# Attention scores from scaled fp16 halves, and one size bound for latent and context inputs

## The chip, the cores and the metric

The kernel runs on one core of one Trainium2 chip. The metric is the time of one execution on the device in microseconds; of several runs the median is taken. Engine names in profile rows: PE is TensorE's matmul, PEld its weight load, DVE VectorE, ACT ScalarE, POOL GpSimd, SP SyncE, which issues DMAs.

## The reference

One layer of a diffusion backbone over 1024 latent tokens with a prefix of 256 context tokens, 1024 channels, all inputs and the output in fp32. A modulated RMS norm and one wide projection feed two token mixers; their outputs are gated, merged and projected, and a ConvFFN follows. What the change touches is the attention mixer: 16 query heads of width 64 in 4 groups, each group with one key and one value head, a window of 128 latent tokens to either side, all 256 context keys, and one learned sink logit per head.

```python
q = apply_rope(rms_norm(heads(aq, ATT_HEADS, ATT_HEAD_DIM), q_norm_w[l]), cos, sin)
k = apply_rope(rms_norm(heads(ak, ATT_KV_HEADS, ATT_HEAD_DIM), k_norm_w[l]), cos, sin)
v = heads(av, ATT_KV_HEADS, ATT_HEAD_DIM)
k_ctx = rms_norm(heads(akc, ATT_KV_HEADS, ATT_HEAD_DIM), k_norm_w[l])
v_ctx = heads(avc, ATT_KV_HEADS, ATT_HEAD_DIM)
...
s_lat = jnp.einsum('btkgd,bskd->bkgts', qblk, kblk).astype(jnp.float32) * ATT_SCALE
s_lat = jnp.where(valid, s_lat, NEG_INF)
s_ctx = jnp.einsum('btkgd,bskd->bkgts', qblk, k_ctx).astype(jnp.float32) * ATT_SCALE
p = jax.nn.softmax(jnp.concatenate([s_lat, s_ctx, sink_b], axis=-1), axis=-1).astype(v.dtype)
return (jnp.einsum('bkgts,bskd->btkgd', p[..., :3 * T], vblk)
        + jnp.einsum('bkgts,bskd->btkgd', p[..., 3 * T:3 * T + C], v_ctx))
```

The other mixer is a chunkwise mLSTM in both directions; it, the merge and the ConvFFN follow the attention in time and are not touched.

## The kernel before

**Products.** The kernel reaches fp32 accuracy with narrower products: each operand is split into a high and a low half (`split_from`: ScalarE writes the high half, VectorE subtracts it from the source for the low one), and three products (high-high, high-low, low-high) are summed in PSUM. In some places the halves are in fp32r, a form of fp32 that TensorE multiplies in one pass; in others they are fp16, and then the operand is first multiplied by a factor that keeps it within fp16's range. Weights get their factor from the sum of their squares (`ScaledWeights.square`, `total`, `back`; `f[:, 2:3]` is the factor, `f[:, 4:5]` its inverse together with that of the inputs). The normalised inputs `hT` (latent) get theirs from a bound on their size (`size_bound`, result in `E.hs`), worked out from the modulation vectors.

**Stages.** `stage_startup` loads the modulation weights, normalises context and latent tokens, forms the context keys and values (`context_keys`, `context_values`, `context_squares`) and the mLSTM's context inputs (the loop over `i` in 0..3, tiles `cx`, `kvx`), and prepares the loop's first weights. The order of its instructions is set by a planner that ranks them by estimated times; `issue_after` pins single ones. `stage_attention` is one loop whose order is written out by hand (`manual_schedule`): step `n` projects block `n` of 32 (4 head groups of 8 blocks of 128 queries, tile `pq`), turns block `n-1` (transposes on TensorE, tile `qt`, into `QT` and `KA`/`KB`), forms scores and softmax of block `n-3` (`Scores`: `product`, `top`, `exps`, `low` for each of four heads `h`) and multiplies block `n-4`'s probabilities with the values (`po`). Between these stands filler work for TensorE: half a tile of gate projection per step (`g`). GpSimd splits the weights of later steps (`split_pool`) and VectorE sums the modulation rows (`macc`). `stage_mlstm` and `stage_tail` follow; the planner orders them.

**Scores.** The query tile `QT` holds, per head, the high half of 64 channels on 64 partitions and the low half on the other 64; the keys `KA` hold the high half twice and `KB` the low half twice. Two matmuls over 128 partitions (L860, L861) then sum all four products, for up to 384 latent keys; L862 and L863 do the same for 256 context keys with `KcA` and `KcB`. All four have the same stationary slice of `QT`. The result lies in one of two score banks (`s`, 1024 columns each). On it VectorE adds the mask with the row factor `ss` and takes the extreme (`top`, L868), ScalarE exponentiates twice (`exps`, L878 into fp16, L879 in place), and VectorE subtracts the two (`low`, L884), after which the bank is free.

**Factors of a head group.** `weight_back(g)` finishes the factors for group `g` three steps into the group before (group 0 ahead of the loop). It calls `back` (a reciprocal on VectorE, L126, and a product on GpSimd, L127). Then it forms, on GpSimd, the factor `up` that latent and context values of the group share. It is the inverse square root of a sum of the inputs' and the context values' squares (`at.vq`, from `context_squares`); L690 is the power. VectorE takes its reciprocal as `down` (L692). `values_act` and `values_dve` use `upi` to write the value halves; `context_values` uses `up`; `norm_row` uses `down` for the normaliser.

**Handover from startup to loop.** The loop's pools reuse the memory of the startup's pools. A tile waits until what lay there has been read. The gate weights' raw pieces (`fr`, L697) are among the first; their squares (L112) and the sum over partitions on TensorE (L119) stand ahead of the first gate tile.

Of the kernel before, what the change touches and what calls it, by code (L numbers as in the profile page):

```python
# [8 lines left out]
F32 = mybir.dt.float32  # L9
F32R = mybir.dt.float32r  # L10
# [8 lines left out]
P = 128  # L19
D = 1024  # L20
L = 1024
# [279 lines left out]
def attention_setup(E, st):  # L301
# [6 lines left out]
    qw = ap.tile([P, 2, HD], F32, name="qw")  # L308
# [3 lines left out]
    def constants():  # L312
        nc.sync.dma_start(qw[:, 0], A["q_norm_w"].to_broadcast([P, HD]))
        nc.sync.dma_start(qw[:, 1], A["k_norm_w"].to_broadcast([P, HD]))
        nc.gpsimd.tensor_scalar(qw[:, 0], qw[:, 0], -(HD ** -0.5), None, op0=ALU.mult)
# [17 lines left out]
    KcA = ap.tile([P, NKV, NCTX], F32R, name="KcA")  # L333
    KcB = ap.tile([P, NKV, NCTX], F32R, name="KcB")
    Vcf = ap.tile([P, NCB, NKV * HD], F32, name="Vcf")
    vq = ap.tile([P, NKV], F32, name="vq")
    at.__dict__.update(maskA=maskA, nsink=nsink, sink=sink, qw=qw, TA=TA, TB=TB, KcA=KcA, KcB=KcB, Vcf=Vcf, vq=vq, constants=constants, tables=tables)
# [3 lines left out]
def stage_startup(E, at):  # L341
# [3 lines left out]
    with ExitStack() as st:  # L345
# [128 lines left out]
        def k_stack(kf, nh, name):  # L474
            w = nh * HD
            kk = wp.tile([P, 512], F32, tag="kk", name=f"kk{name}", bufs=1)
            kh = kk[:, : 2 * w].rearrange("p (h r d) -> p h r d", r=2, d=HD)
            kv = kf.rearrange("p (h d) -> p h d", d=HD)
            for r in range(2):
                copy_act(nc, kh[:, :, r].bitcast(F32R), kv)  # L480
            kl = wp.tile([P, 512], F32, tag="kl", name=f"kl{name}", bufs=1)
            kl4 = kl[:, : 2 * w].rearrange("p (h r d) -> p h r d", r=2, d=HD)
            for r in range(2):
                nc.vector.tensor_tensor(kl4[:, :, r].bitcast(F32R), kv, kh[:, :, r], op=ALU.subtract)
            return kk, kl

# [44 lines left out]
        def context_squares():  # L531
            q = sp.tile([P, NKV], F32, name="vsq")
            for g in range(NKV):
                junk = sp.tile([P, P], F32, name=f"vj{g}", tag="vj").rearrange("p (a b) -> p a b", a=2)
                nc.scalar.activation(junk, at.Vcf[:, :, g * HD : (g + 1) * HD], AF.Square, accum_out=q[:, g : g + 1])
            pb = tp_tile("vq")
            nc.tensor.matmul(pb[:, :NKV], E.ones, q, start=True, stop=True)
            nc.vector.tensor_scalar(at.vq, pb[:, :NKV], 2.0 ** -30, None, op0=ALU.mult)

        def context_keys():  # L540
            for c in range(NCB):
# [13 lines left out]
                nc.vector.tensor_tensor(kv4, kv4, at.qw[:, 1, None, :].to_broadcast([P, NKV, HD]), op=ALU.mult)  # L555
                kk, kl = k_stack(kf, NKV, f"c{c}")
                for src, dst in ((kk, at.KcA), (kl, at.KcB)):
                    pt = tp_tile(f"kct{c}")
                    for h in range(NKV):
                        nc.tensor.transpose(pt[:, h * P : (h + 1) * P], src[:, h * P : (h + 1) * P], ident)  # L560
                    copy_act(nc, dst[:, :, c * P : (c + 1) * P], pt.rearrange("p (h t) -> p h t", h=NKV))


        cs = sp.tile([P, NB, HD], F32, name="cs")
        for i in range(4):
# [48 lines left out]
            if i == 2:  # L614
                context_squares()
# [17 lines left out]
def stage_attention(E, st, at):  # L633
# [44 lines left out]
    def weight_back(g):  # L678
        f = RAW["wf", g]
        if g:  # L680
            w2.back(f)
        if g >= NKV:
            return
        t = wp.tile([P, 8], F32, tag="vs", name=f"vs{g}")
        inv = f[:, 4:5]
        nc.gpsimd.tensor_tensor(t[:, 0:1], inv, inv, op=ALU.mult)
# [3 lines left out]
        nc.gpsimd.tensor_tensor(t[:, 3:4], t[:, 2:3], expo[:, 0:1], op=ALU.pow)  # L690
        nc.gpsimd.tensor_tensor(t[:, 4:5], t[:, 3:4], inv, op=ALU.mult)
        nc.vector.reciprocal(t[:, 5:6], t[:, 3:4])  # L692
        G[g] = dict(inv=inv, inv2=t[:, 1:2], up=t[:, 3:4], upi=t[:, 4:5], down=t[:, 5:6])
# [58 lines left out]
    def values_act(g, b, ps):  # L752
# [3 lines left out]
        copy_act(nc, G[g]["V"][:, b, 0:HD], ps[:, 320:384], scale=G[g]["upi"])  # L756
        return sq

    def values_dve(g, b, ps, sq):
# [5 lines left out]
        nc.gpsimd.tensor_scalar(ss[:, :5], ss[:, :5], G[g]["inv"], None, op0=ALU.mult)  # L765
        V = G[g]["V"]
        nc.vector.scalar_tensor_tensor(
            V[:, b, HD:P], ps[:, 320:384], G[g]["upi"], V[:, b, 0:HD], op0=ALU.mult, op1=ALU.subtract
# [1686 lines left out]
```

## Time and profile before

| what | value |
|---|---|
| median of 3 runs | 1868.58 us (1866.38 to 1869.55) |
| profiled execution, its own time | 1870.95 us |
| its span, first to last instruction | 1869.2 us |
| instructions | 28015 |
| mean granted TensorE clock | 0.985 |
| attention loop, first to last score product | 137.7 to 614.5 us |
| score products L860 to L863 | 128 of each |
| fp32r weight load of `QT` / fp16 weight load of `hH` | 0.19 us / 0.10 us |

A row of instructions gives start, duration, engine, line, operation, the tiles written and read, shapes, and in brackets the idle time of the engine before it with what ended it. A row of groups gives a count, then the busy time in us and the mean of one in ns. Durations of matmuls overlap one another, so the pace of TensorE is read from starts.

### The profile page before, as it was taken

To read this page: it belongs to the slowest core of one execution; us is meant where nothing else is said; L and a number is where in the kernel's file an instruction comes from. 1 tells how busy PE (TensorE), PEld (TensorE's weight loads), DVE (VectorE), ACT (ScalarE), POOL (GpSimd) and SP (SyncE) were. 2 spreads that over 40 slices of the span, in tenths; PEclk is the share of its full clock that TensorE was granted. 3 is DMA by queue.
4 is the path that set the end of the run, shared out by engine and by line. 5 is a ranking of instruction groups with operands and counts; after the bars stand their busy time and mean duration, and the time that the engine had idled before them with its cause. 6 is when DMAs were issued, how large, how long until landed. Compare 5 with 4: busy or idle time off the path is not lost.

```text
span 1869.2 us, 28015 instructions
## 1 busy us (share of the span) xinstructions
PE 1802.4 (96%) x9217; PEld 1317.5 (70%) x9217; DVE 1419.8 (76%) x2870; ACT 1073.5 (57%) x2235; POOL 510.8 (27%) x750
## 2 busy tenths in 40 slices
PE   7889999999999799999999999999999999999999
PEld 3855555656665465757567887878888888888887
DVE  3847878777788585858687888689988898897665
ACT  4846777777777565554455564375544444455441
POOL 2476859577772530403020021000000000000000
PEclk9999999999999999998999999999999999999999
DMA  9646979978786826161439935422455444599751
GB/s 361 217 133 125 186 163 182 198 150 191 167 168 127 218 63 225 35 229 57 158 103 354 377 129 209 180 68 102 175 189 199 172 177 156 193 316 363 278 169 68
DMA packets 302194, 342.49 MB, mean 183 GB/s; under 512 B 176208, under 2 KB 200672, under 8 KB 299232
## 3 DMA queue, kind: packets, MB, share of 16 engines
q1 hardware_dynamic: 287648, 314.47, 55.9%
q10 hardware_dynamic: 14400, 26.22, 4.3%
q8 instruction: 73, 1.20, 0.3%
q14 instruction: 73, 0.60, 0.1%
HBM read 224.61 MB, written 76.16 MB: 161 GB/s over the span
## 4 chain that ended last, share of the span: by engine, by line
PE 79%; DVE 6%; issue 4%; ACT 4%; DMA 3%; POOL 3%; ACTq 0%; SPq 0%; POOLq 0%; DVEq 0%
PE g L724 8%; PE pq L724 7%; PE pa L2033 4%; PE pa L2034 4%; PE pa L2035 4%; PE po L724 3%; PE dx L2033 2%; PE dx L2035 2%; PE dx L2034 2%; PE pb L2034 2%; PE pb L2033 2%; PE pb L2035 2%; PE yb L2033 2%; PE yb L2034 2%; PE yb L2035 2%
## 5 line engine op out<-in xcount | busy, mean ns | idle before, releaser
L868 DVE CUSTOM_DVE_ANT_0 s<-s,maskA,nsink 128x640 f32<-128x640 f32 (+1 forms) x128 | 117.5, 918 | 84.4 <-PE s L863 83.7
L884 DVE TENSOR_TENSOR P<-s,P 128x640 f16<-128x640 f32 (+1 forms) x128 | 100.6, 786 | 0.8 <-ACT s L879 0.8
L878 ACT ACTIVATE P<-s,st 128x640 f16<-128x640 f32 (+1 forms) x128 | 98.2, 767 | 4.2
L724 PE MATMUL g<-hH,fh 128*128 128x512 f16 x256 | 98.3, 384 | 0.0
L724 PE MATMUL g<-hH,fl 128*128 128x512 f16 x256 | 98.0, 383 | 0.0
L724 PE MATMUL g<-hL,fh 128*128 128x512 f16 x256 | 97.8, 382 | 0.0
L879 ACT ACTIVATE s<-s,st 128x640 f32<-128x640 f32 (+1 forms) x128 | 93.8, 733 | 0.0
L876 ACT ACTIVATE st<-st,shift 128x1 f32<-128x1 f32 x128 | 37.6, 294 | 97.7 <-DVE st L868 96.7
L724 PEld LDWEIGHTS <-hH 128*128 128x128 f16 x640 | 60.6, 99 | 38.2 <-issue 2.9
L724 PE MATMUL pq<-wha,hH 128*128 128x384 f16 (+1 forms) x256 | 85.8, 335 | 0.0
L724 PE MATMUL pq<-wla,hH 128*128 128x384 f16 (+1 forms) x256 | 85.7, 335 | 0.0
L724 PE MATMUL pq<-wha,hL 128*128 128x384 f16 (+1 forms) x256 | 85.6, 334 | 0.0
L724 PEld LDWEIGHTS <-fh 128*128 128x128 f16 x512 | 45.9, 99 | 48.0 <-issue 1.6
L1442 POOL TENSOR_SCALAR kwh<-k,gcall 128x128 fp32r<-128x128 f32 x72 | 32.5, 455 | 166.2 <-ACT k L47 41.6
L2171 ACT ACTIVATE cv<-ua,vecT 128x1024 f32<-128x1024 f32 x22 | 27.4, 1245 | 86.2 <-DVE ua L2144 86.2
L860 PE MATMUL s<-KA,QT 128*128 128x384 f32 (+1 forms) x128 | 61.0, 477 | 10.8 <-DVE P L884 8.2
L2033 PE MATMUL dx<-dwh,dfh 128*128 128x512 f32 (+1 forms) x176 | 68.3, 388 | 0.0
L2035 PE MATMUL dx<-dwh,dfl 128*128 128x512 f32 (+1 forms) x176 | 68.3, 388 | 0.0
L2034 PE MATMUL dx<-dwl,dfh 128*128 128x512 f32 (+1 forms) x176 | 68.2, 387 | 0.0
L47 ACT ACTIVATE dfh<-drf 128x512 fp32r<-128x512 f32 x55 | 34.3, 628 | 58.5 <-PE dy L2034 25.6
L163 PE MATMUL kv<-whkv,hH 128*128 128x384 f16 x192 | 62.6, 326 | 4.7 <-DVE VL L56 4.7
L54 DVE TENSOR_TENSOR dfl<-drf,dfh 128x512 fp32r<-128x512 f32 x55 | 37.5, 688 | 34.3 <-ACT dfh L47 34.3
(694 smaller groups left out, 6335.5 us busy)
## 6 DMA issues: line engine op xcount, KB each, us to landing
ur<-in_w_up SPq DMA_DIRECT2D x22, 1024.0 KB
wmb<-in_w_modB SPq DMA_DIRECT2D x48, 256.0 KB
f_d<-cv SPq DMA_DIRECT2D x22, 512.0 KB
wm<-in_w_modA SPq DMA_DIRECT2D x16, 512.0 KB
fr<-in_w_g SPq DMA_DIRECT2D x32, 256.0 KB
drf<-fs_d SPq DMA_DIRECT2D x15, 512.0 KB
drw<-wt_d SPq DMA_DIRECT2D x14, 512.0 KB
w1b<-in_w_cx SPq DMA_DIRECT2D x16, 388.0 KB
```

The lines of the kernel that those rows point to most:

```text
L54: rest = nc.vector.tensor_tensor(lo, src, whole, op=ALU.subtract)
L163: nc.tensor.matmul(ps, lh[:, ls], rh[:, rs], start=start and i == 0, stop=False)
L724: nc.tensor.matmul(self.ps, x, w, start=self.i == 0, stop=self.i == self.n - 1)
L860: nc.tensor.matmul(s[:, self.lat], q, G[g]["KA"][:, ks], start=True, stop=False)
L868: nc.vector.tensor_tensor_reduce(e, e, self.mask, scale=self.ss[:, h : h + 1], scalar=nsink[:, hh : hh + 1], op0=ALU.add, op1=ALU.min, acc ...
L876: nc.scalar.activation(m, st4[:, 8 + h : 9 + h], AF.Identity, bias=shift)
L878: nc.scalar.activation(two[:, :W], e, AF.Exp, bias=m, scale=-1.0)
L879: nc.scalar.activation(e, e, AF.Exp, bias=m, scale=-1.0, accum_out=st4[:, 4 + h : 5 + h])
L884: nc.vector.tensor_tensor(two[:, W : 2 * W], self.e[h], two[:, :W], op=ALU.subtract)
L2033: nc.tensor.matmul(ps, lh, rh, start=start and i == 0, stop=False, skip_group_check=True)
L2034: nc.tensor.matmul(ps, lh, rl, start=False, stop=False, skip_group_check=True)
L2035: nc.tensor.matmul(ps, ll, rh, start=False, stop=stop and i == n - 1, skip_group_check=True)
```

## The change

Queries and keys become fp16 halves, the norm weights get factors for that in `constants`, the size bound covers context inputs as well, and the value factor no longer depends on the context values' squares.

- `constants` forms `wn`: sums of squares of the two norm weights (two ScalarE squares), their inverse square roots on GpSimd (a power over two columns), half the product of the two, and its reciprocal (VectorE). The query and key norm weights are multiplied with these and powers of two; `qw[:, 2]` is the one for context keys.
- `KcA`, `KcB`, `KA`, `KB` and `QT` are fp16 instead of fp32r. `context_keys` no longer stacks two fp32r halves and transposes both; it transposes the keys once and splits them out of PSUM with `split_from`.
- `size_bound` runs over 16 columns instead of 8 (scales and shifts of latent and context).
- `context_squares` and `at.vq` are gone. `weight_back` forms four small products on GpSimd; the power L690 and the reciprocal L692 are gone. The value scale `upi` becomes the constant 2^-15, and the row factor uses `invc`, which holds the norm weights' factor.

```diff
-    qw = ap.tile([P, 2, HD], F32, name="qw")
+    qw = ap.tile([P, 3, HD], F32, name="qw")
+    wn = ap.tile([P, 8], F32, name="wn")
...
-        nc.gpsimd.tensor_scalar(qw[:, 0], qw[:, 0], -(HD ** -0.5), None, op0=ALU.mult)
+        for i in range(2):
+            nc.scalar.activation(qw[:, 2], qw[:, i], AF.Square, accum_out=wn[:, i : i + 1])
+        nc.gpsimd.tensor_scalar(wn[:, 0:2], wn[:, 0:2], 1.0, 1e-36, op0=ALU.mult, op1=ALU.add)
+        nc.gpsimd.tensor_tensor(wn[:, 2:4], wn[:, 0:2], E.expo[:, 0:2], op=ALU.pow)
+        nc.gpsimd.tensor_scalar(wn[:, 4:5], wn[:, 2:3], wn[:, 3:4], 0.5, op0=ALU.mult, op1=ALU.mult)
+        nc.vector.reciprocal(wn[:, 5:6], wn[:, 4:5])
+        nc.gpsimd.tensor_scalar(qw[:, 0], qw[:, 0], wn[:, 2:3], -(2.0 ** -15), op0=ALU.mult, op1=ALU.mult)
+        nc.gpsimd.tensor_scalar(qw[:, 2], qw[:, 1], wn[:, 3:4], 2.0 ** 11, op0=ALU.mult, op1=ALU.mult)
+        nc.gpsimd.tensor_scalar(qw[:, 1], qw[:, 2], wn[:, 4:5], None, op0=ALU.mult)
...
-    KcA = ap.tile([P, NKV, NCTX], F32R, name="KcA")
-    KcB = ap.tile([P, NKV, NCTX], F32R, name="KcB")
+    KcA = ap.tile([P, NKV, NCTX], F16, name="KcA")
+    KcB = ap.tile([P, NKV, NCTX], F16, name="KcB")
...
-            sc = mods[:, 0].rearrange("p k -> p k")
-            nc.gpsimd.tensor_tensor(q[:, 8:16], sc, sc, op=ALU.mult)
-            nc.scalar.activation(q[:, 24:32], q[:, 8:16], AF.Square, accum_out=q[:, 0:1])
-            nc.scalar.activation(q[:, 24:32], mods[:, 2], AF.Square, accum_out=q[:, 1:2])
+            sc, sh = [mods[:, i : i + 2].rearrange("p s k -> p (s k)") for i in (0, 2)]
+            nc.gpsimd.tensor_tensor(q[:, 8:24], sc, sc, op=ALU.mult)
+            nc.scalar.activation(q[:, 24:40], q[:, 8:24], AF.Square, accum_out=q[:, 0:1])
+            nc.scalar.activation(q[:, 24:40], sh, AF.Square, accum_out=q[:, 1:2])
...
-                kk, kl = k_stack(kf, NKV, f"c{c}")
-                for src, dst in ((kk, at.KcA), (kl, at.KcB)):
-                    pt = tp_tile(f"kct{c}")
-                    for h in range(NKV):
-                        nc.tensor.transpose(pt[:, h * P : (h + 1) * P], src[:, h * P : (h + 1) * P], ident)
-                    copy_act(nc, dst[:, :, c * P : (c + 1) * P], pt.rearrange("p (h t) -> p h t", h=NKV))
+                kk = wp.tile([P, 512], F32, tag="kk", name=f"kkc{c}", bufs=1)
+                for r in range(2):
+                    copy_act(nc, kk.rearrange("p (h r d) -> p h r d", r=2, d=HD)[:, :, r], kv4)
+                pt = tp_tile(f"kct{c}")
+                for h in range(NKV):
+                    nc.tensor.transpose(pt[:, h * P : (h + 1) * P], kk[:, h * P : (h + 1) * P], ident)
+                cs_ = slice(c * P, (c + 1) * P)
+                split_from(nc, at.KcA[:, :, cs_], at.KcB[:, :, cs_], pt.rearrange("p (h t) -> p h t", h=NKV))
...
-            if i == 2:
-                context_squares()
...
-        nc.gpsimd.tensor_tensor(t[:, 0:1], inv, inv, op=ALU.mult)
-        nc.gpsimd.tensor_scalar(t[:, 1:2], t[:, 0:1], 1.0 / HD, None, op0=ALU.mult)
-        nc.gpsimd.tensor_scalar(t[:, 2:3], t[:, 0:1], 2.0 ** 30, at.vq[:, g : g + 1], op0=ALU.mult, op1=ALU.add)
-        nc.gpsimd.tensor_scalar(t[:, 2:3], t[:, 2:3], 1e-36, None, op0=ALU.add)
-        nc.gpsimd.tensor_tensor(t[:, 3:4], t[:, 2:3], expo[:, 0:1], op=ALU.pow)
-        nc.gpsimd.tensor_tensor(t[:, 4:5], t[:, 3:4], inv, op=ALU.mult)
-        nc.vector.reciprocal(t[:, 5:6], t[:, 3:4])
-        G[g] = dict(inv=inv, inv2=t[:, 1:2], up=t[:, 3:4], upi=t[:, 4:5], down=t[:, 5:6])
+        nc.gpsimd.tensor_scalar(t[:, 0:1], inv, inv, 1.0 / HD, op0=ALU.mult, op1=ALU.mult)
+        nc.gpsimd.tensor_tensor(t[:, 1:2], inv, at.wn[:, 5:6], op=ALU.mult)
+        nc.gpsimd.tensor_scalar(t[:, 2:3], f[:, 2:3], E.hs[:, 0:1], 2.0 ** -15, op0=ALU.mult, op1=ALU.mult)
+        nc.gpsimd.tensor_scalar(t[:, 3:4], inv, 2.0 ** 15, None, op0=ALU.mult)
+        G[g] = dict(inv=inv, inv2=t[:, 0:1], invc=t[:, 1:2], up=t[:, 2:3], down=t[:, 3:4])
...
-                KA=kp.tile([P, L], F32R, tag="KA", name=f"KA{g}"),
-                KB=kp.tile([P, L], F32R, tag="KB", name=f"KB{g}"),
+                KA=kp.tile([P, L], F16, tag="KA", name=f"KA{g}"),
+                KB=kp.tile([P, L], F16, tag="KB", name=f"KB{g}"),
...
-        copy_act(nc, G[g]["V"][:, b, 0:HD], ps[:, 320:384], scale=G[g]["upi"])
+        copy_act(nc, G[g]["V"][:, b, 0:HD], ps[:, 320:384], scale=2.0 ** -15)
...
-        QT = wp.tile([P, 512], F32R, tag="QT", name=f"QT{g}_{b}", bufs=3)
+        QT = wp.tile([P, 512], F16, tag="QT", name=f"QT{g}_{b}", bufs=3)
```

More of the change, by code (lines that the diff above doesn't have):

```diff
@@ L331, in tables @@
                 nc.gpsimd.tensor_tensor(TB[i][:, :, 32:64], sinb, w1, op=ALU.mult)
-    KcA = ap.tile([P, NKV, NCTX], F32R, name="KcA")
-    KcB = ap.tile([P, NKV, NCTX], F32R, name="KcB")
+    KcA = ap.tile([P, NKV, NCTX], F16, name="KcA")
+    KcB = ap.tile([P, NKV, NCTX], F16, name="KcB")
     Vcf = ap.tile([P, NCB, NKV * HD], F32, name="Vcf")
-    vq = ap.tile([P, NKV], F32, name="vq")
-    at.__dict__.update(maskA=maskA, nsink=nsink, sink=sink, qw=qw, TA=TA, TB=TB, KcA=KcA, KcB=KcB, Vcf=Vcf, vq=vq, constants=constants, tables=tables)
+    at.__dict__.update(maskA=maskA, nsink=nsink, sink=sink, qw=qw, TA=TA, TB=TB, KcA=KcA, KcB=KcB, Vcf=Vcf, wn=wn, constants=constants, tables=tables)
     return at
@@ L472, in stage_startup @@
         size_bound()
[L474 to L485, printed above, removed]
         def both(ps, w, n, ks):
@@ L529, in context_values @@
                     copy_act(nc, at.Vcf[:, c], pvc[c][:, :256])
[L531 to L538, printed above, removed]
         def context_keys():
```

10 lines of the change are left out of this document (5 added, 5 removed).

## The prediction

> **What bounds the kernel now.** I read the page first, then the stages by windows, then the waits inside the attention loop, then the instructions around the longest of them.
>
> ```profile
> span 1869.2 us, 28015 instructions
> ...
> PE 1802.4 (96%) x9217; PEld 1317.5 (70%) x9217; DVE 1419.8 (76%) x2870; ACT 1073.5 (57%) x2235; POOL 510.8 (27%) x750
> ...
> PE 79%; DVE 6%; issue 4%; ACT 4%; DMA 3%; POOL 3%; ACTq 0%; SPq 0%; POOLq 0%; DVEq 0%
> ```
>
> TensorE is busy for 96% of the span and carries 79% of the chain that ended last. So a microsecond counts where TensorE stands still, or where its own work gets shorter; the rest is hidden until it makes TensorE wait. The windows cut the span into startup, attention loop and everything after it (columns: length, busy time and count of PE, PEld, DVE, ACT and POOL, granted clock, DMA share, GB/s).
>
> ```profile
> 0.00:137.70 137.70, 114.20 (x629) 79.62 (x629) 77.18 (x159) 76.74 (x160) 61.89 (x94) 0.94 0.68 239
> 137.70:614.50 476.80, 459.11 (x2638) 279.96 (x2637) 372.94 (x962) 362.57 (x908) 327.37 (x402) 0.99 0.80 166
> 614.50:1869.20 1254.70, 1229.11 (x5955) 957.88 (x5953) 969.70 (x1750) 634.15 (x1168) 121.50 (x255) 0.99 0.52 184
> ```
>
> The change touches the first two stages. In the loop TensorE idles 476.8 - 459.1 = 17.7 us. The waits of that stage (us in total, times, longest) say what ends the idle time:
>
> ```profile
> DVE vs L692 <- POOL vs L690: 9.4, 3, 3.2
> ...
> PE s L860 <- DVE P L884: 8.2, 6, 2.0
> ```
>
> Both are one event, seen three times, once for each head group prepared inside the loop. `weight_back` ends in a reciprocal on VectorE (L692) of a power that GpSimd computes (L690). VectorE takes its work in order, so while the reciprocal waits, the score maximum behind it (L868) and the subtraction that frees a score bank (L884) stand too, and TensorE finds no bank. The middle event in time order (start, duration, and in brackets the idle time before):
>
> ```profile
> 270.99 0.15 DVE L126 RECIPROCAL wfa<-wfa 128x1 f32<-128x1 f32 x1
> 274.31 0.16 DVE L692 RECIPROCAL vs<-vs 128x1 f32<-128x1 f32 x1 [3.17 <-POOL vs L690]
> 274.43 0.82 DVE L868 CUSTOM_DVE_ANT_0 s<-s,maskA,nsink 128x512 f32<-128x512 f32 x1
> ...
> 272.44 0.19 POOL L686 TENSOR_TENSOR vs<-wfa 128x1 f32<-128x1 f32 x1
> ...
> 273.70 0.57 POOL L690 TENSOR_TENSOR vs<-vs,expo 128x1 f32<-128x1 f32 x1
> ...
> 271.10 0.28 PE L863 MATMUL s<-KcB,QT 128*128 128x256 f32 x1
> ...
> 276.00 0.41 PE L860 MATMUL s<-KA,QT 128*128 128x384 f32 x1 [2.02 <-DVE P L884]
> ...
> 153.44 0.66 PE L860 MATMUL s<-KA,QT 128*128 128x384 f32 x1 [1.99 <-DVE P L884]
> ...
> 393.81 0.41 PE L860 MATMUL s<-KA,QT 128*128 128x384 f32 x1 [2.01 <-DVE P L884]
> ```
>
> The reader is to see that the scores of the last head were ready at 271.10 + 0.28 = 271.4, that VectorE began on them at 274.43, and that TensorE lost 2.0 us each time. There is a second price, in the granted clock (column behind the five busy times):
>
> ```profile
> 152.80:159.60 6.80, 6.16 (x20) 3.64 (x21) 4.33 (x12) 4.16 (x10) 5.57 (x5) 0.50 0.75 157
> 272.30:275.70 3.40, 1.69 (x8) 0.59 (x6) 1.39 (x4) 0.32 (x2) 2.42 (x8) 1.00 0.16 40
> 391.75:395.20 3.45, 1.44 (x10) 1.11 (x10) 3.08 (x10) 2.01 (x5) 2.03 (x5) 1.00 0.09 18
> 395.20:398.60 3.40, 3.40 (x13) 1.80 (x12) 2.41 (x6) 2.17 (x6) 3.25 (x4) 0.50 0.94 245
> ```
>
> After the first and third stall TensorE worked at half clock, for 6.8 and 3.4 us.
>
> **The change part by part.** (a) *The factor of a head group (`weight_back`).* Six GpSimd instructions with a power become four without one, and no reciprocal follows on VectorE. The remaining reciprocal, L126 of `back`, had its input long before (0.15 us, no wait). VectorE then reaches L868 at about 271.4 instead of 274.43, the bank is freed 3.0 us earlier, and TensorE's 2.0 us are covered: 3 x 2.0 = **6.0 us**. The next thing late would be the scores themselves, TensorE's own work. The GpSimd queue also gets shorter, by about 1 us: from 272.44 to the power's end at 274.27 it runs five instructions and one more follows, against four short ones. The bound below is a gain of 0, if another operand of L868 came as late; its operands are the scores at 271.4, mask and sink from before the loop, and the row factors of an earlier step.
>
> (b) *The half clock behind the stalls.* Of 6.16 us busy at half clock half is lost, 3.1 us, and 1.7 of 3.4: together **4.8 us**. Ends: 0, if the clock falls for another reason, and 4.8. I take 4.8, since in both cases the idle stretch stands right ahead. The second stall was not followed by it, and the two windows say why it may not have been: TensorE was busy 1.69 us of the 3.4 before 275.7, and only 1.44 before 395.2. [...]
>
> (c) *The score products in fp16.* `Scores.product` issues four matmuls a head with the same stationary slice of `QT`. A typical block:
>
> ```profile
> 302.24 0.38 PE L724 MATMUL g<-hL,fh 128*128 128x512 f16 x1
> ...
> 304.40 0.38 PE L724 MATMUL g<-hH,fl 128*128 128x512 f16 x1
> 304.43 0.53 PE L860 MATMUL s<-KA,QT 128*128 128x384 f32 x1
> ...
> 305.09 0.28 PE L863 MATMUL s<-KcB,QT 128*128 128x256 f32 x1
> 305.21 0.34 PE L724 MATMUL pq<-wha,hH 128*128 128x384 f16 x1
> ...
> 307.33 0.33 PE L724 MATMUL pq<-wla,hH 128*128 128x384 f16 x1
> ...
> L861 PEld LDWEIGHTS s<-KB,QT 128*128 128x128 f32 x128 | 24.5, 192 | 2.1
> L724 PEld LDWEIGHTS <-hH 128*128 128x128 f16 x640 | 60.6, 99 | 38.2 <-issue 2.9
> ...
> 600.00:610.00 10.00, 8.65 (x58) 5.55 (x59) 9.93 (x19) 6.06 (x18) 9.59 (x7) 1.00 0.47 102
> ```
>
> Durations overlap, so starts are read. Ten 512-column fp16 products take 2.16 us, 0.216 each; thirteen of 384 columns (305.21 to 307.33) 2.12, 0.163 each. That is 0.41 ns a column, so 256 columns of fp16 would take 0.11. The block takes 305.21 - 304.40 - 0.216 = 0.594 us; in fp16 it would be 2 x 0.163 + 2 x 0.11 = 0.546. So today's format already streams at nearly the same rate, and the gain is 0.048 us a head, the 256-column products (0.12 each now) giving less than half of it. A quarter of the heads, first and last block of a group, have four 256-column products, for 4 x 0.01; so 0.045 on average. A weight load of fp16 takes 99 ns against 192 and would no longer be longer than the product it hides behind. All 128 heads would give 5.8 us; the last three steps (12 heads) lie where VectorE is full (9.93 of 10 us), so I count 116: **5.2 us**. Ends: 0, if what precedes a block and not the format costs the difference, and 128 x 0.06 = 7.7 us, if the block came down to its bare 1280 columns (0.53 us).
>
> (d) *ACT and VectorE in the loop.* The copies into `QT` and `KA` and the subtractions into `QT` and `KB` keep their count and shape and still read fp32 from PSUM; a scale that was a tile becomes a constant. I take 0; both engines have 100 us of idle time in this stage to cover a small change either way.
>
> (e) *Startup.* These rows carry it:
>
> ```profile
> L535 ACT ACTIVATE vj<-Vcf 128x128 f32<-128x128 f32 x4 | 1.2, 306 | 0.0
> L47 ACT ACTIVATE KcB<-kct 128x512 fp32r<-128x512 f32 x2 | 1.2, 592 | 0.0
> L484 DVE TENSOR_TENSOR klc<-kcf,kkc 128x256 fp32r<-128x256 f32 x4 | 1.5, 418 | 0.0
> 142.51 0.69 DVE L884 TENSOR_TENSOR P<-s,P 128x512 f16<-128x512 f32 x1
> 28.17 0.40 POOL L315 TENSOR_SCALAR qw<-qw 128x64 f32<-128x64 f32 x1 [12.84 <-DMA qw<-in_q_norm_w]
> 29.37 0.59 ACT L47 ACTIVATE mrow<-pm 2x512 f32<-2x512 f32 x1 [5.65 <-PE pm L455]
> ...
> 103.20 0.86 SPq L628 DMA_DIRECT2D vx_d<-kvx  x2
> 107.00 1.76 SPq L697 DMA_DIRECT2D fr<-in_w_g  x4
> ...
> 110.42 0.63 ACT L112 ACTIVATE wjg<-fr 128x512 bf16<-128x512 f32 x1
> 111.19 0.59 PE L119 MATMUL pq<-wqg,ones 128*128 128x2 f32 x2 [6.22 <-ACT wjg L112]
> ```
>
> Removed: four squares and two copies on ACT (2.4 us, off a queue that is also used for the x blocks), four subtractions on VectorE (1.5 us), eight transposes. Added: two subtractions out of PSUM (2 x 0.69 = 1.4), two small ACT squares, six short GpSimd instructions for one and a reciprocal on VectorE, all ahead of the first use of `qw`, where GpSimd idled. The squares wait for `qw`, which landed at 28.2; if they stand ahead of the copy of `mrow` at 29.37 and k's vector lands late, that copy and all of startup shift by up to 1 us. Between -2.4 and +1 I take -0.5. The smaller tiles also move what the loop's first buffers fall on: by the tile sizes in order of their pools, the first piece of a gate weight (`fr`) no longer lies on the `kvx` rows whose write to DRAM ends at 107.0, the second still does. So one of the two squares that TensorE waits for until 111.19 can come early, 0.7 us at most; I take **1.0 us** for startup and handover together. The wider `size_bound` adds eight columns to three tiny instructions: 0, covered by the idle GpSimd; its cost without cover would be some tens of ns.
>
> **The sum.** 6.0 + 4.8 + 5.2 + 1.0 = 17.0 us. The profiled execution took 1870.95 us around its span of 1869.2, so 1854.0; it is 2.4 us above the median shown, 1868.58. As the half clock depends on where a stall falls, the median may hold less of it, so the forecast stays at **1854 us**, 14.6 below it.
>
> **The rivals.** *Stalls go, the half clock stays* (another cause, or the clock falls elsewhere): 1854 + 4.8 = 1859; for it speaks the middle stall, which had none, against it the two others. Chance 0.15. [...] *The score blocks gain nothing* (an fp16 product of 256 columns still paces at 0.12, as no row shows one): 1854 + 5.2 = 1859; against it speaks 0.163 for 384 columns, where the load is as long. Chance 0.13, and 0.04 for both together, 1864. *The change does not do what it says*: VectorE, past the reciprocal, waits for something else, and the freed time comes back as longer waits for scores, leaving startup (1.0) and a third of the blocks (1.7): 1868.6 - 2.7, about 1866. The loop's DMA share of 0.80 speaks for it a little, the 22% idle time of VectorE against. Chance 0.07. *More than the sum*: TensorE's 137.7 - 114.2 = 23.5 us of idle time in startup shrink by a quarter as well: 1854 - 6 = 1848, chance 0.07. *Slower*: the order of everything after the loop is planned from estimated durations, and those before it change. TensorE idles there 1254.7 - 1229.1 = 25.6 us; were that doubled by a worse order, the time would be 1880. It decides only from 14.6 + 3.7 = 18.3 us of new idle time on. Against it: no instruction of those stages changes, and the loop's own order is written by hand. Chance 0.04.
>
> **How the numbers follow.** The likeliest case has 0.50 and gives 1854. The first five cases that end faster sum to 0.89; the absorbed gain is within 0.2% (0.07), which is 3.7 us and about what this measurement can tell from no change; slower has 0.04. The range goes from 1847 (the case of more than the sum, less a little) to 1863 (one of the two losses and 4 us of startup beside it). It leaves out both losses together, the absorbed gain and the slower case, 0.15 in all, and some of the edges.
>
> **What would show it.** No L692 or its like waiting in VectorE, L868 within 0.5 us of the scores at the three places; the wait of the first score product for L884 down from 8.2 to about 2 us; clock 1.00 behind them; starts of the context products 0.11 apart and loads of 0.1 us; a loop of about 461 us instead of 476.8. I am wrong if a new wait of VectorE or a half-clock stretch stands in the loop, if fp16 blocks still take 0.59 us, or if startup ends later than now.

## The result, and the profile after

| | before | after |
|---|---|---|
| median | 1869.07 us (1866.38 to 1871.23, 4 runs) | 1853.38 us (1852.30 to 1858.65, 4 runs) |
| ratio of the times | | 0.9922 (95%: 0.9899 to 0.9946) |
| profiled execution, its span | 1870.95, 1869.2 us | 1858.65, 1856.9 us |
| loop, first to last score product | 476.8 us | 459.0 us |

The median fell by 15.7 us and lies 0.6 us from the forecast of 1854. The profiled execution of the changed kernel was the longest of its four, 5 us above the median; the loop does not carry that, as a second profile shows further down. One run in eight of a kernel further down (c6_fill) took 3508.66 us at a mean clock of 0.90 and is left out of its median. The windows of the same three stages:

```profile
0.00:139.60 139.60, 117.57 (x618) 80.88 (x619) 75.89 (x157) 75.10 (x154) 62.48 (x97) 0.93 0.68 236
139.60:598.60 459.00, 446.96 (x2640) 250.85 (x2639) 371.58 (x958) 360.18 (x908) 324.95 (x396) 1.00 0.82 172
598.60:1856.90 1258.30, 1230.64 (x5953) 954.30 (x5951) 971.16 (x1750) 635.45 (x1168) 123.13 (x255) 0.99 0.52 183
```

All of the gain is in the loop: 17.8 us shorter, 12.2 of them TensorE's busy time (459.11 to 446.96) and 5.6 its idle time (17.7 to 12.0). The clock there is 1.00 instead of 0.99. The stages around it are 1.9 and 3.6 us longer in this one execution.

TensorE's waits inside the loop, in us: total, times, longest. The first row stood at 8.2, 6, 2.0 before; none of its six waits now lies at the three places, and five of them (3.3 us) lie in the loop's last steps.

```profile
PE s L842 <- DVE P L866: 3.9, 6, 1.1
PE pq L882 <- DVE wfg L120: 3.3, 12, 0.5
PE po L706 <- DMA T<-P: 2.9, 3, 2.1
```

The place of the second event, in time order of each engine. Line 126 is the reciprocal of `back`, L850 is the score maximum (L868 before), L671 to L674 are the four products of `weight_back`:

```profile
265.78 0.15 DVE L126 RECIPROCAL wfa<-wfa 128x1 f32<-128x1 f32 x1
266.22 0.82 DVE L850 CUSTOM_DVE_ANT_0 s<-s,maskA,nsink 128x512 f32<-128x512 f32 x1 [0.28 <-PE s L845]
...
265.91 0.27 PE L845 MATMUL s<-KcB,QT 128*128 128x256 f16 x1
...
267.33 0.26 POOL L671 TENSOR_SCALAR vs<-wfa 128x1 f32<-128x1 f32 x1
...
268.15 0.23 POOL L674 TENSOR_SCALAR vs<-wfa 128x1 f32<-128x1 f32 x1
```

The window around it (columns as above):

```profile
262.00:272.00 10.00, 10.00 (x59) 5.63 (x58) 8.62 (x24) 7.03 (x17) 5.60 (x12) 1.00 0.85 146
```

The scores are ready at 265.91 + 0.27 = 266.18 and the maximum starts at 266.22: VectorE waits for the scores, and no longer for GpSimd, whose four products run from 267.33 on with nobody behind them. TensorE works for 10.00 of 10.00 us. A score block between two gate products now:

```profile
290.20 0.38 PE L706 MATMUL g<-hL,fh 128*128 128x512 f16 x1
290.42 0.33 PE L842 MATMUL s<-KA,QT 128*128 128x384 f16 x1
290.58 0.33 PE L843 MATMUL s<-KB,QT 128*128 128x384 f16 x1
290.75 0.27 PE L844 MATMUL s<-KcA,QT 128*128 128x256 f16 x1
290.86 0.27 PE L845 MATMUL s<-KcB,QT 128*128 128x256 f16 x1
290.96 0.38 PE L706 MATMUL g<-hH,fl 128*128 128x512 f16 x1
```

Its weight load among the groups (busy us, mean ns, idle time before):

```profile
L842 PEld LDWEIGHTS <-QT 128*128 128x128 f16 x128 | 12.9, 101 | 16.8 <-DVE P L866 6.9
```

It takes 290.96 - 290.20 - 0.216 = 0.544 us (0.594 before), its context products start 0.11 apart, and a load takes 0.10 us.

### The profile page after: what moved, and what is told of

Read it like the earlier page. It is cut to its first block, busy times and chain, and to the rows that moved or that the text cites. A ratio compares the mean times of both kernels' runs of the same rounds, so it can differ in the third digit from the quotient of the medians.

```text
span 1856.9 us, 27874 instructions
## 1 busy us (share of the span) xinstructions
PE 1795.2 (97%) x9207; PEld 1286.0 (69%) x9207; DVE 1418.6 (76%) x2864; ACT 1070.7 (58%) x2229; POOL 510.5 (27%) x747
## 4 chain that ended last, share of the span: by engine, by line
PE 77%; DVE 7%; DMA 5%; ACT 5%; issue 4%; POOL 3%; ACTq 0%; SPq 0%; POOLq 0%; DVEq 0%
PE g L706 8%; PE pq L706 6%; PE pa L2015 4%; PE pa L2017 4%; PE pa L2016 4%; PE po L706 3%; PE dx L2015 2%; PE dx L2017 2%; PE dx L2016 2%; PE pb L2017 2%; PE pb L2016 2%; PE pb L2015 2%; PE yb L2015 2%; PE yb L2016 2%; PE yb L2017 2%
## 5 line engine op out<-in xcount | busy, mean ns | idle before, releaser
L850 DVE CUSTOM_DVE_ANT_0 s<-s,maskA,nsink 128x640 f32<-128x640 f32 (+1 forms) x128 | 117.5, 918 | 75.0 <-PE s L845 74.6
L866 DVE TENSOR_TENSOR P<-s,P 128x640 f16<-128x640 f32 (+1 forms) x128 | 100.7, 787 | 1.0 <-ACT s L861 1.0
L164 PE MATMUL kv<-wlkv,hH 128*128 128x384 f16 x192 | 63.2, 329 | 0.4
```

The costliest lines, as they stand in the source:

```text
L164: nc.tensor.matmul(ps, lh[:, ls], rl[:, rs], start=False, stop=False)
L850: nc.vector.tensor_tensor_reduce(e, e, self.mask, scale=self.ss[:, h : h + 1], scalar=nsink[:, hh : hh + 1], op0=ALU.add, op1=ALU.min, acc ...
L866: nc.vector.tensor_tensor(two[:, W : 2 * W], self.e[h], two[:, :W], op=ALU.subtract)
```

## The experiments

Stage lengths come from the profile of each; "half clock" is the time in which the granted clock of TensorE was 0.5. In the clock records of before and after, its stretches inside the span last 3.41 us or two, three or four times as long.

| kernel | median us | ratio to before (95%) | loop us | TensorE idle in it | half clock in it |
|---|---|---|---|---|---|
| before | 1869.07 | 1 | 477.1 | 17.7 | 10.2 |
| x0_after: the change again | 1852.77 | 0.9912 (0.9898 to 0.9926) | 459.2 | 12.7 | 0 |
| c1_no_wait | 1862.55 | 0.9966 (0.9954 to 0.9979) | 467.0 | 12.6 | 0 |
| c2_fp32r | 1859.44 | 0.9952 (0.9939 to 0.9965) | 465.3 | 10.7 | 0 |
| c3_wait_back | 1863.00 | 0.9965 (0.9951 to 0.9978) | 469.4 | 19.3 | 6.8 |
| c4_pool_only | 1854.74 | 0.9914 (0.9885 to 0.9942) | 459.8 | 12.8 | 0 |
| c5_short_wait | 1857.22 | 0.9927 (0.9900 to 0.9953) | 463.1 | 14.5 | 3.4 |
| c6_fill | 1862.16 | 0.9960 (0.9945 to 0.9976) | 469.1 | 14.7 | 3.4 |
| c7_long_wait | 1873.99 | 1.0022 (1.0011 to 1.0033) | 480.3 | 27.0 | 17.1 |
| v1_total_late | 1846.90 | 0.9875 (0.9852 to 0.9899) | 462.9 | 13.3 | 6.8 |
| v2_turn_first | 1843.26 | 0.9860 (0.9837 to 0.9883) | 454.2 | 6.8 | 0 |

(Here the loop ends with the end of the last score product, 0.3 us later than in the window of 476.8 us.)

**The change once more (x0_after).** No edit.

> The changed kernel once more, as the yardstick for the others and for what a stage varies by. If the loop's gain belongs to the change, its length from the first to the last score product is again 459.0 us within 1 us. If the 1.9 us that startup was longer in the first profile are only the granted clock (20.4 us at half clock against 17.0 before, worth 1.7 us), startup lies anywhere between 136 and 141 us; if they belong to the change, it is 139 us or more again. Time 1852 to 1858 us.

Measured: loop 459.2 us, startup 136.8 instead of 139.6, everything after the loop 1256.8. So the loop repeats within 0.2 us, and the 1.9 us that startup had grown are no property of the change. The reason offered for them does not hold in that form: both profiles of the changed kernel have 20.5 us of half clock in startup. What repeats is TensorE's idle time there, 21.9 and 22.0 us.

**The wait alone (c1_no_wait).** The kernel before, one line:

```diff
-        nc.vector.reciprocal(t[:, 5:6], t[:, 3:4])
+        nc.gpsimd.tensor_tensor(t[:, 5:6], t[:, 2:3], t[:, 3:4], op=ALU.mult)
```

> The kernel before, with the reciprocal L692 taken off VectorE: the same factor is formed on GpSimd as a product of two columns that it holds already. Formats, startup and order stay. Theory (terms a and b of the prediction): no 2.0 us idle time of TensorE at the three places, 6.0 us, and no half clock behind them, up to 4.8 us: loop 466 to 467 us instead of 476.8, time 1858 to 1860 us. Rival 1, the stall is absorbed (something else is late there): loop 475 us or more, time 1867 or more. Rival 2, the half clock does not come from the stalls: loop about 471 us, time 1863.

Windows around the three places:

```profile
148.00:158.00 10.00, 9.27 (x58) 6.30 (x58) 7.59 (x27) 7.36 (x19) 7.99 (x16) 1.00 0.82 160
260.00:272.00 12.00, 11.74 (x69) 6.87 (x68) 9.89 (x29) 8.56 (x24) 6.72 (x17) 1.00 0.78 136
378.00:390.00 12.00, 12.00 (x69) 7.34 (x68) 10.24 (x27) 8.91 (x25) 7.66 (x16) 1.00 0.82 185
```

The waits of the loop for score banks that remain:

```profile
PE s L860 <- DVE st L895: 3.5, 2, 2.1
...
PE s L860 <- DVE P L884: 2.0, 3, 0.8
```

Moving one 0.16 us instruction to another engine shortens the loop by 10.1 us, with no half clock in it. Laid beside the trace of before, TensorE's products come 2.1, 2.4 and 2.2 us earlier at the three places (6.8 together) and another 3.0 and 1.5 behind the first and third, where the clock had been halved (4.5). About 1.1 us are lost again to other waits of the last steps, where VectorE was busy for 9.93 of 10 us before. By the loop and its clock both rivals fall. The time does not decide as clearly: 1862.55 us misses the 1858 to 1860 expected and lies where the second rival had it (1863). The medians differ by 6.4 us only; the stages outside the loop were 5 us longer in the profile of this kernel, and its profiled execution is 3.5 us above its median.

**The format alone (c2_fp32r).** The changed kernel with `QT`, `KA`, `KB`, `KcA` and `KcB` as before:

```diff
-        QT = wp.tile([P, 512], F16, tag="QT", name=f"QT{g}_{b}", bufs=3)
+        QT = wp.tile([P, 512], F32R, tag="QT", name=f"QT{g}_{b}", bufs=3)
...
```

> The changed kernel with QT, KA, KB, KcA and KcB in fp32r again, all else as changed. Theory (term c): only the score blocks grow, by 0.045 us for each of 116 to 128 heads: loop 459.0 + 5.2 to 5.8 = 464.2 to 464.8 us, time about 1858.7 us. Rival, the blocks' gain is covered where VectorE or the buffers set the pace: loop below 462 us. Rival, the heavier weight loads (0.19 against 0.10 us) cost elsewhere too: loop above 467 us. Startup against the kernel of c1 shows what the fewer transposes are worth: theory 0 to 1 us.

The same block as above in this kernel:

```profile
289.23 0.38 PE L706 MATMUL g<-hL,fh 128*128 128x512 f16 x1
289.26 0.52 PE L842 MATMUL s<-KA,QT 128*128 128x384 f32 x1
289.62 0.34 PE L843 MATMUL s<-KB,QT 128*128 128x384 f32 x1
289.80 0.28 PE L844 MATMUL s<-KcA,QT 128*128 128x256 f32 x1
289.92 0.28 PE L845 MATMUL s<-KcB,QT 128*128 128x256 f32 x1
290.04 0.39 PE L706 MATMUL g<-hH,fl 128*128 128x512 f16 x1
```

And its weight load:

```profile
L842 PEld LDWEIGHTS s<-KA,QT 128*128 128x128 f32 x128 | 24.3, 190 | 16.6 <-issue 2.7 <-PE po L706 1.8 <-PE g L706 1.2
```

The block is back at 290.04 - 289.23 - 0.216 = 0.594 us, the loop at 465.3, so the format is worth 465.3 - 459.2 = 6.1 us there, and 6.7 us in the medians; the loop is 0.5 us longer than the most that was expected. A block with 384-column products gains 0.050 us here (0.048 in the median) and one of four 256-column products 0.040 (medians 0.476 and 0.436). That is about 0.011 us a product, nearly the same for either width. Five blocks that follow a run of one-column sums (L288) gain more, 0.12 to 0.15 us each. Startup ends at 137.0 us, 2.2 earlier than in c1, where 0 to 1 was expected for the fewer transposes; as startup ends anywhere from 136.1 to 139.6 us in kernels that share it, this does not tell their worth.

**The wait put back (c3_wait_back).** The changed kernel with a chain of the old shape:

```diff
-        nc.gpsimd.tensor_scalar(t[:, 3:4], inv, 2.0 ** 15, None, op0=ALU.mult)
+        nc.gpsimd.tensor_tensor(t[:, 4:5], inv, inv, op=ALU.mult)
+        nc.gpsimd.tensor_scalar(t[:, 4:5], t[:, 4:5], 2.0 ** 30, None, op0=ALU.mult)
+        nc.gpsimd.tensor_tensor(t[:, 5:6], t[:, 4:5], expo[:, 0:1], op=ALU.pow)
+        nc.vector.reciprocal(t[:, 3:4], t[:, 5:6])
```

> The changed kernel with a wait like that at L692 put back: a column of the factors is squared, scaled and raised to a power on GpSimd, and VectorE takes its reciprocal. Three more GpSimd instructions and one reciprocal for each of four head groups; fp16 scores stay. Theory: VectorE stands 3 us at three places, TensorE 2 us each, loop 459.0 + 6.0 = 465 us without half clock behind the stalls, up to 470 us with it; time 1859 to 1864 us. Rival, the wait was harmful only together with the slower fp32r blocks: loop below 461 us. For the clock: half clock should follow only where TensorE was busy for less than about 0.6 of the 3.41 us before it, and always where it was busy for less than 0.36.

The waits of VectorE and of TensorE:

```profile
DVE vs L677 <- POOL vs L676: 9.8, 3, 3.3
...
PE s L845 <- DVE P L869: 11.7, 8, 2.2
```

Windows of 3.4 us before and behind each of the three stalls (the clock is the third number from the end):

```profile
147.80:151.20 3.40, 1.54 (x12) 1.19 (x10) 1.28 (x4) 0.25 (x1) 2.44 (x8) 0.99 0.01 1
151.20:154.60 3.40, 3.08 (x11) 1.53 (x12) 2.71 (x10) 2.79 (x8) 2.48 (x3) 0.50 0.57 104
267.20:270.60 3.40, 1.33 (x7) 0.44 (x6) 1.75 (x6) 0.69 (x2) 2.07 (x6) 1.00 0.29 77
270.60:274.00 3.40, 3.40 (x13) 1.69 (x12) 3.33 (x10) 2.96 (x8) 2.89 (x3) 0.50 0.74 145
386.60:390.00 3.40, 1.89 (x13) 1.18 (x14) 3.40 (x10) 2.32 (x6) 1.79 (x3) 1.00 0.23 44
390.00:393.40 3.40, 3.40 (x24) 2.31 (x23) 3.37 (x9) 3.09 (x9) 3.25 (x4) 1.00 0.97 262
```

The loop grows by 10.2 us, the size of what c1 had taken away, now with fp16 scores: the wait costs the same in either format. The median, 1863.00, is 10.2 us above that of x0. This time it is the first and second stall that half clock follows (1.54 and 1.33 us busy before), not the third (1.89). The limits of the expectation, 0.36 and 0.6, lie near what the traces of before and after show: divided at the changes of the granted clock into steps of 3.41 us, they have half clock behind all nine steps at full clock in which TensorE was busy for under 0.40, and behind none in which it was busy for over 0.60. The fullest step that it followed has 2.04 us (149.41 us in before), the emptiest that it did not 1.44 us (803.26 us after).

**The chain without the wait (c4_pool_only).** As c3, but the last factor stays on GpSimd:

```diff
-        nc.vector.reciprocal(t[:, 3:4], t[:, 5:6])
+        nc.gpsimd.tensor_tensor(t[:, 3:4], t[:, 4:5], t[:, 5:6], op=ALU.mult)
```

> As the kernel of c3, but the last factor is a product on GpSimd instead of VectorE's reciprocal: GpSimd's chain is as long as there (square, scale, power, one more), and VectorE waits for none of it. Theory: what costs is VectorE standing in its queue, not the length of GpSimd's chain: loop 459 to 460 us as in the changed kernel, time about 1853 us. Rival, GpSimd's longer chain makes something else late (the row factors or the weight splits behind it): loop 461 us or more.

Loop 459.8 us, median 1854.74. GpSimd's chain may be as long as it was; VectorE standing for it is what costs.

**A shorter and a longer wait (c5_short_wait, c7_long_wait).** In c5 the reciprocal takes the third GpSimd result; in c7 the chain of c3 is longer by seven instructions.

```diff
-        nc.gpsimd.tensor_scalar(t[:, 3:4], inv, 2.0 ** 15, None, op0=ALU.mult)
+        nc.vector.reciprocal(t[:, 3:4], t[:, 2:3])
```

> The changed kernel with the last factor as VectorE's reciprocal of the third GpSimd result (which holds just its inverse) instead of GpSimd's fourth product: one wait of VectorE per group, but a short one, about 2 us instead of 3.3. Theory: TensorE has about 1 us of cover (3.0 to 3.3 us of VectorE's wait became 2.0 to 2.4 of TensorE's), so it loses about 1 us three times: loop 459.1 + 3 = 462 us, and in the 3.41 us around each stall TensorE stays busy for about 0.7, so no half clock: time about 1856 us. Rival, any wait there costs as much as the long one: loop 465 us or more. Rival, a wait this short is covered: loop 460 us or less.

> The kernel of c3 with seven more GpSimd instructions in the chain that VectorE waits for, some 2.5 us longer: VectorE waits 5.8 us. Theory: TensorE loses VectorE's wait less 1.1 us (3.17 gave 2.0, 3.3 gave 2.2, 2.1 gave 1.1), so 4.7 us at three places, 14 us, and half clock follows each of them, since TensorE is busy for less than 0.4 of some 3.41 us there: 3 times 1.7 to 3.4 us more: loop 459.2 + 14 + 5 to 10 = 478 to 483 us, time 1872 to 1877 us. Rival, a longer wait meets other slack (the other score bank, filler products): loop below 474 us.

VectorE's wait and TensorE's in c5:

```profile
DVE vs L674 <- POOL vs L673: 6.4, 3, 2.2
PE s L842 <- DVE P L866: 6.6, 7, 1.1
```

The same two in c7:

```profile
DVE vs L682 <- POOL vs L681: 16.9, 3, 5.7
PE s L850 <- DVE P L874: 14.1, 4, 4.6
```

And c7's windows behind the three stalls:

```profile
152.00:158.80 6.80, 4.42 (x15) 2.14 (x16) 5.29 (x15) 4.18 (x10) 5.09 (x7) 0.50 0.46 99
274.90:281.70 6.80, 4.75 (x16) 2.40 (x17) 5.30 (x15) 4.18 (x10) 5.04 (x7) 0.50 0.52 128
397.70:401.10 3.40, 3.40 (x12) 1.66 (x13) 3.25 (x11) 2.89 (x8) 2.81 (x3) 0.51 0.63 129
```

Both rows take the longest waits, which need not belong to one event. Event by event, VectorE's waits of 2.04, 3.16 and 5.55 us at the first place (c5, c3, c7) cost TensorE 1.05, 2.18 and 4.57; those of 2.17, 3.30 and 5.68 at the second cost 0.94, 2.07 and 4.45, and the third place agrees with the second. So 1.0 us is covered at the first place and 1.2 at the other two (1.0 to 1.2 before), and every microsecond beyond is paid in full. c5 loses 3.9 us in the loop (about 1 us more than expected, with 3.4 us of half clock at its end, not behind one of these stalls); c7 loses 21.1 and ends slower than the kernel before, as forecast.

**Filler during the stall (c6_fill).** c3 with products that nobody reads ahead of the score product that stalls:

```diff
+            if n in (4, 12, 20):
+                dm = tp_tile(f"dm{n}")
+                x, w = hT[0][0], W1[seq[n][0]][0][0]
+                for _ in range(12):
+                    nc.tensor.matmul(dm[:, :384], x[:, 0:P], w[:, :384], start=True, stop=True)
```

> The kernel of c3 (wait put back), with 12 products of 384 columns that nobody reads (0.163 us each, 2.0 us together) on TensorE ahead of the first score product of steps 4, 12 and 20, where TensorE stands 2.0 to 2.2 us. If the half clock behind the stalls comes from TensorE having too little work in its 3.41 us, it is gone with the filler, while the stall's own time stays: loop 459.2 + 6.5 = 465.7 us (466 at most) against 469.4 with the same wait and no filler, no half clock between 150 and 460 us, time about 1859 to 1860 us. Rival, the half clock follows from something else that happens there (VectorE's or GpSimd's state, a load on memory): half clock behind one or more of the three places again and a loop of 467.5 us or more.

The one wait of the filler:

```profile
PE dm L1147 <- DVE m L290: 2.8, 1, 2.8
```

Windows: the first place (before the filler starts, and behind), then a stretch around the second and around the third:

```profile
151.50:154.90 3.40, 0.73 (x7) 0.66 (x7) 2.09 (x9) 1.02 (x3) 1.80 (x5) 1.00 0.00 0
154.90:158.30 3.40, 3.24 (x11) 1.51 (x11) 0.11 (x2) 1.30 (x4) 3.20 (x4) 0.50 0.73 163
268.80:278.80 10.00, 9.88 (x56) 5.23 (x55) 6.70 (x22) 5.68 (x15) 6.21 (x14) 1.00 0.53 81
384.00:396.00 12.00, 11.88 (x71) 6.69 (x69) 8.01 (x24) 6.78 (x16) 7.31 (x14) 1.00 0.45 100
```

At the second and third place it went as expected: TensorE is busy through the stall, the clock stays at 1.00 and only 2.2 us are lost each time. At the first the filler itself had no PSUM bank: its buffer was still held by a VectorE instruction (L290) behind the same reciprocal, so TensorE stood 2.8 us, half clock followed, and the loop came to 469.1 instead of 465.7 us. By its letter that is the rival's result (half clock behind one place, a loop above 467.5), and what speaks for the theory are the two places that the filler did fill. Two places are few, as half clock followed only four of the six stalls of 2.0 to 2.2 us before and in c3; the count over all traces, below, carries more.

**Two steps further (v1_total_late, v2_turn_first).** The handover's wait is still the longest one at the loop's start (4.8 us of TensorE), and L882 waits 15 times for VectorE in the loop. v1 puts the squares, the sum and the factor of the second gate weight at the end of step 0; v2 also puts `norm_turn` ahead of the sums:

```diff
...
             gate.some(24)
+            if not n:
+                gate_total(1, ps[:, 464:466])
+                gate_back(1)
...
+            if prior:
+                prior.norm_turn(ps)
             for kind, c in totals(n) if n else ():
                 (gate_total(c, ps[:, 464:466]) if kind == "g" else weight_total(c, ps[:, 472:476]))
-            if prior:
-                prior.norm_turn(ps)
```

> The changed kernel with the handover from startup to loop mended: in step 0 the squares of the second gate weight, its sum on TensorE and the factor stand at the end of the step, behind the first gate tile (24 products of 0.216 us, 5.2 us) instead of ahead of it. Theory: TensorE no longer stands 4.8 us for a square that waits for the weight's DMA, most of it is covered: first score product 3 to 5 us earlier, about 1 us more where no half clock follows; time 1848 to 1850 us. Rival, the wait only moves (the turning of the first block waits for ScalarE, which the late squares hold up): gain below 1.5 us.

> As v1, and in every step with a weight's sum the transposes of the row sums (L882) stand ahead of that sum on TensorE, so that they need not wait until VectorE has read it (15 waits of 0.25 us in the loop). Theory: 3.5 to 4 us of idle time in the loop go: loop 455 to 456 us without the handover's part, time 1845 to 1847 us. Rival, the transposes then wait for VectorE's row sums instead, as long: loop as in v1.

In v1 the gate products follow the projection without a gap, where TensorE had stood for 4.8 us:

```profile
105.20 0.33 PE L706 MATMUL pq<-wha,hL 128*128 128x400 f16 x1
105.37 0.38 PE L706 MATMUL g<-hH,fh 128*128 128x512 f16 x1
```

The window of v2's loop:

```profile
134.40:588.60 454.20, 447.39 (x2641) 248.91 (x2640) 370.94 (x959) 359.91 (x908) 324.76 (x396) 1.00 0.82 174
```

v1 begins its scores at 131.3 us (136.8 in x0) and takes 1846.9; its half clock in startup is 6.8 us instead of 20.5. v2, with the same startup, begins them at 134.4 us with 13.7 us of half clock, so only a part of v1's 5.5 us belongs to the edit; what both show is TensorE's idle time in startup, 19.5 and 19.2 us against 21.9. v2's loop is 454.2 us, the waits of L882 are gone, and at 1843.26 us it beats both kernels; v1 and v2 ended 1.1 and 1.7 us below the ranges expected of them. v2 is 26.2 us below the runs of before that were taken with it (1869.48), 9.5 below x0. v1's profile has two half-clock stretches of 3.4 us in the last steps of the loop, worth up to 3.4 of the 3.7 us by which its loop is longer than x0's.

## Why the prediction was right, point by point

| term | predicted us | measured us | from |
|---|---|---|---|
| (a) stalls | 6.0 | 6.8 | c1: 2.1 + 2.4 + 2.2 |
| (b) half clock behind them | 4.8 | 4.5 | c1: 3.0 + 1.5 |
| (c) fp16 score blocks | 5.2 | 6.1 | c2 against x0, loop |
| (d) ScalarE and VectorE | 0 | not separable | |
| (e) startup and handover | 1.0 | idle time 1.5 and 1.6 less | before against after and x0 |
| sum; measured: the whole change | 17.0 | 15.7 (medians; 16.2 with x0), 16.4 (profiles of before and x0) | |

**(a)** held as told: same three places, same queue, and the next thing late is the scores (0.28 us of VectorE's wait). At the second and third place the maximum starts 0.04 us behind the scores; at the first it is 0.71 us, beyond the 0.5 named, as VectorE is still busy with what stands ahead in its queue, and TensorE does not wait for it. The wait of the score products for L884 (now L866), which was to fall to about 2 us, is 3.9, 3.3 of it in the last steps, where score products waited 4.0 us before as well. c1, c3 and c4 show cause and place: taken away alone it gives 10.1 us with (b), put back alone it costs 10.2, and without VectorE in it the same chain costs 0.6 us at most.

**(b)** held in size in the profiles, and the range was right to leave it open: what is lost depends on where a stall falls. Before, stalls one and three were followed by half clock; in c3, one and two. The median of c3 is 10.2 us above that of x0, of which its stalls alone (3 x 2.2) explain 6.6; the medians of before and c1 differ by no more than the stalls' 6.8. So how much half clock the typical run pays stays open.

**(c)** The pace was right (0.546 forecast, 0.544 measured), and so was the narrow block's 0.04. The term was 0.9 us too small. Read by starts between like neighbours, 122 of the heads give 6.0 us, 0.049 each instead of 0.045, since five of them follow the one-column sums and gain 0.12 to 0.15. That the last steps would not pay was right: c2's lag behind x0 is 6.7 us larger at x0's 547 us than at the loop's start, and 6.1 at its end.

**(d)** The KB subtraction takes 291 ns before and after, and the waits of the two engines that appeared are single ones of 0.7 us or less. Of the loop's 17.9 us (before against x0), 10.1 came with the wait (c1) and 6.1 with the format (c2); the remaining 1.7 lie between c1 (467.0) and c2 (465.3), about 0.3 us behind each of the second and third place and most of the rest in the last steps. The prediction had no term for them, and their cause was not separated.

**(e)** The feared shift of `mrow` did not come: the copy starts at 29.38 us, 29.37 before. In the handover the first piece moved as told, but that is not what shortened TensorE's wait. SP's rows before and after (start, duration):

```profile
103.20 0.86 SPq L628 DMA_DIRECT2D vx_d<-kvx  x2
107.00 1.76 SPq L697 DMA_DIRECT2D fr<-in_w_g  x4
...
106.46 0.86 SPq L613 DMA_DIRECT2D vx_d<-kvx  x2
107.38 3.52 SPq L679 DMA_DIRECT2D fr<-in_w_g  x4
```

In the changed kernel the first piece is issued right behind the write of `vx_d` instead of 2.9 us later; the second still waits for that write. TensorE's wait for the squares is 4.4 to 5.0 us in the eight profiles with the changed startup and 5.9 and 6.2 in the two with the old one: 1.3 us, more than the 0.7 given as its most. But one of the eight, c2, with `KcA` and `KcB` as large as before, still issues its first piece 2.0 us behind the row of the write (106.14 us), and its wait is 5.0 us all the same; the other seven have 4.7 in the mean. So the early piece is worth about 0.3 us, and what took off the other 1 us stays open. The ends of the whole stage say less: startup varies from 136.1 to 139.6 us over the same eight.

**The rivals.** "Half clock stays" fell with c1, "blocks gain nothing" with c2, "absorbed" with c1 and c4. "Slower by a new plan" did not come: TensorE idles 27.6 and 25.1 us behind the loop in the two profiles, 25.6 before. "More than the sum" did not come with this change; v1 and v2 show that startup had some of it to give.

**By luck.** Between the profiles of before and x0 the loop gave 17.9 us where (a) to (c) had 16.0, startup 0.9 where (e) had 1.0, and the stages behind the loop, put at 0, took back 2.4 us (1256.8 against 1254.4). That the total came within about 1 us of the forecast is partly luck: a loop that gave 1.9 us too much met a loss that was not foreseen. In x0 there are 4.4 us more of half clock behind the loop (31.7 against 27.3), which would be worth 2.2 us; but the first profile of the changed kernel took 3.8 us longer there (1258.2) with 27.3 us of it, as before, so the cause of the loss is not shown.

## What to carry to other kernels

VectorE, which ran its queue in order here, held up all that stood behind a reciprocal of 0.16 us while that waited for 2.0 to 5.7 us (c5, c3, c7): look for waits of the engine that frees buffers, measure how much of such a wait the bound engine covers (here 1.0 to 1.2 us), and move the tiny instruction to the engine that makes its input (c1: the loop 10.1 us shorter). One line did more than half of this change's work in the loop by the profiles (10.1 of 17.9 us), and 6.4 of 16.2 us of the whole time by the medians. Read a format's gain from starts between like neighbours, since it may be a fixed sum for each instruction and not a rate (here about 0.011 us a product at 256 and at 384 columns). Where TensorE's idle time is cut, look at the granted clock behind it too; and compare stages rather than whole times: the two profiles of the changed kernel agree to 0.2 us in the loop and differ by 4.1 us in the span.

## What the runs showed of the hardware

In the clock records of before and after, every stretch at full or half clock that ends inside the span lasts a whole multiple of 3.41 us: at half clock one to four such steps (3.41, 6.83, 10.24, 13.65 us), at full clock four to 259 (13.65 to 884.05 us). At half clock the 384-column products of c3 start 0.32 us apart (270.6 to 273.9 us), at full clock 0.163.

Cutting the twelve traces along these steps and taking TensorE's busy share in each: half clock followed all 65 steps at full clock in which it was busy for under 0.40, 20 of 40 at 0.40 to 0.50, 18 of 55 at 0.50 to 0.62, 4 of 34 at 0.62 to 0.70 and none of 216 at 0.70 to 0.90. In before and after alone it is 9 of 9, 3 of 9, 5 of 12, 0 of 4 and 0 of 41. The steps are not all independent, as the twelve kernels share most of their stages, and between 0.40 and 0.70 the busy share alone does not decide. Nor does the length of a gap: in the startup of the first changed profile a step with gaps of 0.62, 0.57 and 0.37 us (69.40 us, 0.54 busy) was followed by half clock, and one with 1.44 us of a single gap (42.09 us, 0.58 busy) was not. Of the stalls of 2.0 to 2.2 us before and in c3, the two that lay wholly within a step left 0.39 and 0.41 and were followed by half clock, and of the four that fell across two steps (0.46 to 0.60 left) two were: four of the six in all. The steps do not start with the program: counted from the first instruction, their edges lie about 2.6 us behind a multiple of 3.41 us before and 1.1 us in the first changed profile. That a stall falls differently in them from run to run is the author's estimate; what the runs show is that the mean clock of one kernel varies (0.983 to 0.989 in the 17 runs of before that were taken with c6 and c7).

An fp32r product of 256 or 384 columns costs about 0.011 us more than one in fp16 here (256 columns start 0.12 apart in c2, 0.11 in the changed kernel, one matmul record to a product in both), with a load of 0.19 us against 0.10; which of the two, load or product, makes the difference was not separated.
